# A hybrid decoder step on one core: keys of both attention maps split in one operation, and a later place for one group's weight loads

## The chip, the core and the metric

The kernel runs on one core of a Trainium2 chip. A core has five engines with instruction streams of their own: TensorE (matrix products; PE in the profile, its weight loads PEld), VectorE (DVE), ScalarE (ACT), GpSimd (POOL) and SyncE (SP), which here only issues transfers. SyncE, ScalarE and POOL can issue DMA transfers, each on a queue of its own; 16 DMA engines move the data. Each stream is worked off in order, and an instruction that waits for a semaphore holds all that stands behind it in its stream. The metric is the device time of one execution in microseconds (us), as the median of several runs. The profile is of one further execution.

## The reference

One layer of a decoder for 1024 prompt tokens and 8 sample tokens, model width 1024, all in float32: a mixer of differential attention (4 heads) and retention (4 heads) with one input and one output projection, a cross-attention to 256 memory tokens, a squared-ReLU MLP of width 4096, and a final RMSNorm. Two places matter here.

```
q1, q2 = q[..., :64], q[..., 64:]          # a head's 128 columns hold two maps
k1, k2 = k[..., :64], k[..., 64:]
attn = probs(q1, k1) - lam * probs(q2, k2) # two softmax maps, scale and bias inside
oa   = einsum('bhqk,bkhd->bqhd', attn, v)

y = square(relu(h @ w_up)) @ w_down        # hidden width 4096 = 4 groups of 1024
```

## The kernel before

**Precision.** A float32 operand is split into a high part in the format that TensorE takes at full rate (a ScalarE cast) and a low part (a VectorE subtraction, operand minus high part). A product is then high x high, high x low and low x high.

**Attention of the prompt.** TensorE's instructions are kept in the order in which they are written. A planner puts those of the other engines, transfers too, in an order by its own estimates of when each is ready; `issue_after(x)` makes an instruction stand behind x on its engine. The four heads overlap: while the scores of head h are computed, the query and key projection of head h+1 fills gaps on TensorE (`head_proj`, lines 919 to 947; it leaves keys in `kraw` and queries in `qraw`, 64 rows of map 0 above 64 rows of map 1, by 1032 columns). A loop over 44 steps (line 1369), ten to a head, says which scores, transposes and products with values come when.

`load_stacks` (949) takes the tiles of a head, one buffer each: KA[0], KA[1], KB[0], KB[1], Q[0], Q[1], each of 128 rows by 1024 columns. For map m, KA[m] is to hold the high part of the keys of that map in both of its 64-row halves, KB[m] the low part in both, and Q[m] the high part of the queries in one half and their low part in the other. So one product with KA[m] and one with KB[m] make the scores (`scores`, 999). `load_part` (961) fills columns in two calls per head: EARLY (columns 0 to 687, from step 3 of the head before) and LATE (688 to 1023, from step 7). Per map it casts 64 rows into the half of KA[m] in which they already lie, copies that half to the other by a transfer of POOL, and does the same for KB[m] with the subtraction; then both maps of Q follow. It is a generator: four pieces of it are spread over steps 3, 4, 4, 5 and 7, 7, 8, 8. Head 0 is filled ahead of the loop.

SyncE's queue in that stretch holds, in the planner's order, the bias rows of the next head (`M`), the key output, a row of norm factors of the head before and its broadcast (`norm_row`, 1098), the values of the next head, pages of the cache (`ck`), pieces of the input for the output projection (`x_half`), and more. POOL also reloads operands (`UH`, `UL`, line 1436).

**Down projection.** The hidden activations lie in DRAM as HQ and HT. For each of four groups g of 1024 hidden rows (line 2478) the product with the weights is done by seven products of half-size blocks (numbered q: 1, 2, 6, 7, 4, 5, 3), each for four column blocks p and two column chunks c, 12 matmuls of 258 columns each. `right_lower(g, q)` (2369) loads the right operand of product q in two pieces of 516 KB (`raw_h`, a ring of three buffers), casts (2381) and subtracts (2382) them into one of four slots. `load_left` (2489) loads the group's weights, two tiles of 512 KB for each p (`raw_d`, one buffer each), with the eight loads of groups 1 to 3 written ahead of that group's products; `left_lower` (2392) makes the weights of product q from them. `residual_rows` (2358) loads the rows to which results are added (`c`). In group 0 many of these stand behind named instructions; `seen["SP"]` is the last transfer that `right_lower` or `load_left` issued. The loads of group 1 have no such edge: nothing but the planner's estimate says where they go among group 0's transfers.

Of the kernel before, what the change touches and what calls it, by code (L numbers as in the profile page):

```python
# [10 lines left out]
F32 = mybir.dt.float32  # L11
# [37 lines left out]
def decoder_step(ctx: ExitStack, tc: tile.TileContext, i: dict, o: dict):  # L49
    nc = tc.nc  # L50
# [131 lines left out]
    seen = {}  # L182
# [719 lines left out]
    with pool("b") as A:  # L902
# [58 lines left out]
        def load_part(h, cs):  # L961
            KA, KB, Q, _ = stacks[h]
            qraw, kraw = raws[h]
            for m in range(2):
                own = slice(64 * m, 64 * m + 64)
                oth = slice(64 - 64 * m, 128 - 64 * m)
                nc.scalar.copy(KA[m][own, cs], kraw[own, cs])
                nc.gpsimd.dma_start(KA[m][oth, cs], KA[m][own, cs])
                nc.vector.tensor_sub(KB[m][own, cs], kraw[own, cs], KA[m][own, cs].bitcast(F32))
                nc.gpsimd.dma_start(KB[m][oth, cs], KB[m][own, cs])  # L970
                yield
            for m in range(2):
                own = slice(64 * m, 64 * m + 64)
                oth = slice(64 - 64 * m, 128 - 64 * m)
                nc.scalar.copy(Q[m][own, cs], qraw[own, cs])
                nc.vector.tensor_sub(Q[m][oth, cs], qraw[own, cs], Q[m][own, cs].bitcast(F32))
                yield

        vraws = {}
# [311 lines left out]
        for _ in load_part(0, EARLY):  # L1291
            pass
# [76 lines left out]
        for g in range(-4, 40):  # L1369
            h, x = divmod(g, 10)  # L1370
# [6 lines left out]
            if h < 3:  # L1377
                if h >= 0 and x == EARLY_AT[0]:
                    load_stacks(h + 1)
                    until(h + 1, 1, 1)  # L1380
                    early = load_part(h + 1, EARLY)
                for y in (0, 1, 2, 3):
                    if h >= 0 and x == EARLY_AT[y]:
                        if y == 2:
                            until(h + 1, 1, 0)
                        next(early)
                if x == LATE_AT[0]:
                    until(h + 1, 2, 1)
                    late = load_part(h + 1, LATE)
                for y in (0, 1, 2, 3):  # L1390
                    if x == LATE_AT[y]:
                        if y == 2:
                            until(h + 1, 2, 0)
                        next(late)
# [38 lines left out]
            while reloaded[0] < 3 and (3, reloaded[0], 0) in done:  # L1433
                cs = slice(reloaded[0] * CH, reloaded[0] * CH + CH)
# [15 lines left out]
            if g in UNITS_AT:  # L1450
                x = UNITS_OUT[len(us_out) - 1]
# [224 lines left out]
    with pool("d") as A:  # L1676
# [62 lines left out]
        for pr in range(4):  # L1739
            us = [unit(U_MQ + 2 * pr + x) for x in range(2)]  # L1740
            if pr == 0:
                seen["DVE"] = nc.cur_bb.bb.instructions[-1]
                with tc.issue_after(seen["DVE"]):
                    for c in range(2):
                        cs = slice(c * CH, c * CH + CH)
# [6 lines left out]
            for f, c in late + rest if pr else rest + late:  # L1752
                q = qm[2 * pr + f]
                cs = slice(c * CH, c * CH + CH)
# [377 lines left out]
    with pool("e") as A, pool("e_ps", space=PSUM) as PS:  # L2132
# [61 lines left out]
        for n, (ft, c) in enumerate(order):  # L2194
# [4 lines left out]
            cs = QCOLS[c]  # L2199
# [8 lines left out]
            x = xq[ft // 4, c][:, ft % 4, :]  # L2208
# [133 lines left out]
    with pool("acc", side="right") as AC, pool("rd", side="right") as RD, pool("w") as A, pool("w_ps", space=PSUM) as PS:  # L2342
# [135 lines left out]
        for g in range(4):  # L2478
# [10 lines left out]
            def load_left(pairs):  # L2489
                for p in pairs:  # L2490
                    for x in range(2):
                        nc.sync.dma_start(raws[p][x][:, :1024], i["wall"][U_DN + 8 * g + 2 * p + x])
                seen["SP"] = nc.cur_bb.bb.instructions[-1]

            load_left((0, 1) if g == 0 else range(4))
            S, W, bank, copied = {}, {}, {}, {}

            parts = [((1, 2), (1, 2), (0, 1)), ((), (1, 2), (2, 3)), ((6,), (6,), (0, 1)), ((), (6,), (2, 3))]
# [270 lines left out]
```

## Time and profile before

| | |
|---|---|
| time, median of 3 runs | 1474.56 us (1473.46 to 1474.77) |
| profiled execution | 1475.19 us, of which the span of instructions is 1473.4 |
| TensorE busy | 1455.7 us (99%), 11013 matmuls |
| VectorE, ScalarE, POOL busy | 1107.9 (75%), 679.7 (46%), 314.4 us (21%) |
| DMA | 238.98 MB, mean 162 GB/s |
| mean granted TensorE clock | 0.996 of full speed |

Times in the rows are us from the start of the span unless marked ns. A releaser behind `<-` is what ended a wait, by the semaphores. The attention of the prompt lies at about 230 to 430 us, the down projection at 1134 to 1470.

### The profile page before, as it was taken

The numbers are of one execution on the slowest core, as the hardware profiler recorded it, in microseconds if no ns is written. First come the engines' busy times: TensorE is split into PE (matmuls) and PEld (weight loads), VectorE is DVE, ScalarE is ACT, GpSimd is POOL, SyncE is SP. The second block draws the span as 40 slices with busy tenths as digits, with TensorE's granted clock in tenths as the row PEclk, the third lists the DMA queues.
The fourth block names the chain that finished last, engine by engine and source line by source line (L and its number), as shares of the span: only waits on it lengthen the run. The fifth ranks groups of instructions, "written<-read, shape, count | busy, mean of one in ns | idle before, by whom it ended". The sixth has DMA issues, their size and how long they took to land.

```text
span 1473.4 us, 28129 instructions
## 1 busy us (share of the span) xinstructions
PE 1455.7 (99%) x11013; PEld 1401.0 (95%) x11013; DVE 1107.9 (75%) x2263; ACT 679.7 (46%) x1327; POOL 314.4 (21%) x345
## 2 busy tenths in 40 slices
PE   9999999999999999999999999999999999999998
PEld 7899779999889999999999999999999999999998
DVE  7666536888867756567868988888888878787876
ACT  7434435666552441267436533343435443343454
POOL 0035433122304511224122000000002211110380
PEclk9999999999999999999999999999999999999998
DMA  8155738215957265654762444333446764536273
GB/s 295 62 188 171 205 70 192 72 34 159 283 169 269 100 209 170 177 178 122 236 234 77 151 159 158 138 136 133 149 159 216 262 213 144 173 105 200 71 130 116
DMA packets 129833, 238.98 MB, mean 162 GB/s; under 512 B 13606, under 2 KB 80987, under 8 KB 129572
## 3 DMA queue, kind: packets, MB, share of 16 engines
q1 hardware_dynamic: 91354, 170.66, 36.0%
q0 software_dynamic: 27472, 46.93, 11.8%
q10 hardware_dynamic: 10874, 19.60, 3.5%
q8 instruction: 86, 1.41, 0.4%
q14 instruction: 47, 0.39, 0.1%
HBM read 171.13 MB, written 58.92 MB: 156 GB/s over the span
## 4 chain that ended last, share of the span: by engine, by line
PE 88%; DVE 5%; DMA 2%; ACT 2%; issue 1%; POOL 0%; ACTq 0%; SPq 0%; DVEq 0%
PE dn L2412 20%; PE Z L2244 9%; PE qkp L75 6%; PE Y L2244 6%; PE X L2244 6%; PE mq L75 6%; PE pr_m L75 6%; PE pr_o L75 5%; PE grp L75 3%; PE sp L75 2%; PE mv L75 2%; PE mk L75 1%; PE av L75 1%; PE mpv L75 1%; PE vap_z L524 1%; PE vrp_z L524 1%
## 5 line engine op out<-in xcount | busy, mean ns | idle before, releaser
L2412 PE MATMUL dn<-UH,wd 128*128 128x258 f32 (+1 forms) x1800 | 326.6, 283 | 3.0 <-DVE c L2546 3.0
L2412 PEld LDWEIGHTS dn<-UH,wd 128*128 128x128 f32 x1800 | 279.6, 190 | 3.6 <-ACT wd L2388 2.6
L2412 PE MATMUL dn<-UL,wd 128*128 128x258 f32 x900 | 254.6, 283 | 0.0
L2412 PEld LDWEIGHTS dn<-UL,wd 128*128 128x128 f32 x900 | 170.5, 189 | 0.1
L2546 DVE TENSOR_TENSOR c<-c,dn 128x258 f32<-128x258 f32 (+1 forms) x217 | 89.1, 417 | 38.5 <-PE dn L2412 35.8
L2270 ACT ACTIVATE hq<-r 128x258 f32<-128x258 f32 x128 | 53.7, 421 | 117.4 <-DVE r L2269 117.3
L2244 PE MATMUL Z<-T_h,wu 128*128 128x258 f32 x512 | 98.1, 283 | 0.0
L2244 PE MATMUL X<-UH,wu 128*128 128x258 f32 x512 | 97.5, 282 | 0.0
L2388 ACT CAST wd<-raw_d 128x512 fp32r<-128x512 f32 x96 | 58.7, 619 | 82.0 <-PE dn L2412 77.3
L2052 ACT CAST wu<-raw_up 128x512 fp32r<-128x512 f32 x96 | 59.0, 616 | 61.0 <-PE Z L2244 52.6
L2381 ACT CAST UH<-raw_h 128x1032 fp32r<-128x1032 f32 x56 | 58.7, 1055 | 55.2 <-PE dn L2412 27.9
L2244 PEld LDWEIGHTS X<-UH,wu 128*128 128x128 f32 x512 | 81.3, 188 | 0.0
L2244 PEld LDWEIGHTS Z<-T_h,wu 128*128 128x128 f32 x512 | 81.3, 189 | 0.0
L2382 DVE TENSOR_TENSOR UL<-raw_h,UH 128x1032 fp32r<-128x1032 f32 x56 | 72.9, 1301 | 9.9 <-ACT UH L2381 9.9
L2389 DVE TENSOR_TENSOR wd<-raw_d,wd 128x512 fp32r<-128x512 f32 x96 | 72.3, 759 | 10.2 <-ACT wd L2388 10.2
L2281 POOL DMA_DIRECT2D HT<-ht x32 | 17.2, 536 | 292.1 <-DVE ht L2280 291.6
L2244 PE MATMUL Z<-T_l,wu 128*128 128x258 f32 x256 | 72.3, 282 | 0.0
L2244 PE MATMUL X<-UL,wu 128*128 128x258 f32 x256 | 72.3, 282 | 0.0
L129 ACT CAST wh_u<-raw_u 128x1024 fp32r<-128x1024 f32 x43 | 44.7, 1047 | 57.6 <-PE mq L75 39.9
L2053 DVE TENSOR_TENSOR wu<-raw_up,wu 128x512 fp32r<-128x512 f32 x96 | 64.8, 689 | 3.6 <-ACT wu L2052 3.6
L2402 POOL TENSOR_TENSOR raw_d<-raw_d,raw_d 128x512 f32<-128x512 f32 x16 | 22.1, 1384 | 197.0 <-DVE raw_d L2398 145.3
L130 DVE TENSOR_TENSOR wl_u<-raw_u,wh_u 128x1024 fp32r<-128x1024 f32 x39 | 48.6, 1257 | 20.2 <-ACT wh_u L129 20.0
(616 smaller groups left out, 4707.4 us busy)
## 6 DMA issues: line engine op xcount, KB each, us to landing
raw_u<-in_wall SPq DMA_DIRECT2D x49, 512.0 KB
HT<-ht POOLq DMA_DIRECT2D x32, 516.0 KB, 3.0
raw_h<-HT SPq DMA_DIRECT2D x32, 516.0 KB
raw_up<-in_wall SPq DMA_DIRECT2D x32, 512.0 KB
raw_d<-in_wall SPq DMA_DIRECT2D x32, 512.0 KB
HQ<-hq ACTq DMA_DIRECT2D x32, 387.0 KB
raw_h<-HQ SPq DMA_DIRECT2D x24, 516.0 KB
cmk<-in_cmk SPq DMA_DIRECT2D x16, 512.0 KB
```

The source lines that it names most:

```text
L75: pinned(nc.tensor.matmul(out, l, r, start=start, stop=stop))
L130: (lo_engine or nc.vector).tensor_sub(wl[:, :n], raw[:, :n], wh[:, :n].bitcast(F32))
L2052: nc.scalar.copy(w[:, :512], src)
L2053: nc.vector.tensor_sub(w[:, 512:], src, w[:, :512].bitcast(F32))
L2244: pinned(nc.tensor.matmul(ps, l, r[:, k, :], start=first and k == 0 and x == 0, stop=k == 3 and x == 2, skip_group_check=True))
L2270: nc.scalar.activation(h[:, PLACE[quad], :], r, AF.Square)
L2381: nc.scalar.copy(h, rv)
L2382: nc.vector.tensor_sub(l, rv, h.bitcast(F32))
L2388: nc.scalar.copy(w[:, :512], src)
L2389: nc.vector.tensor_sub(w[:, 512:], src, w[:, :512].bitcast(F32))
L2412: pinned(nc.tensor.matmul(ps[:, part], l, r[:, k, cq], start=first and k == 0 and x == 0, stop=k == 3 and x == 2, skip_group_check=True))
L2546: nc.vector.tensor_add(y, y, ps)
```

## The change

In `load_part`, for heads 1 to 3, one cast now fills KA[1] with all 128 rows (map 0's high part in its first half, map 1's in its second, as `kraw` has them), and one subtraction fills KB[1] in the same way. POOL copies the first half of KA[1] into both halves of KA[0], and that of KB[1] into both halves of KB[0]. Then, beside the two pieces that fill Q, SyncE copies the second half of KA[1] over its first, and that of KB[1] over its first. Head 0 is filled as before. In the down projection the eight weight loads of group 1 get an edge behind the last transfer that group 0's last `right_lower` issued.

```
         def load_part(h, cs):
             KA, KB, Q, _ = stacks[h]
             qraw, kraw = raws[h]
-            for m in range(2):
+            lo, hi = slice(0, 64), slice(64, 128)
+            if h:
+                nc.scalar.copy(KA[1][:, cs], kraw[:, cs])
+                for x in (lo, hi):
+                    nc.gpsimd.dma_start(KA[0][x, cs], KA[1][lo, cs])
+                nc.vector.tensor_sub(KB[1][:, cs], kraw[:, cs], KA[1][:, cs].bitcast(F32))
+                yield
+                for x in (lo, hi):
+                    nc.gpsimd.dma_start(KB[0][x, cs], KB[1][lo, cs])
+                yield
+            for m in range(0 if h else 2):
                 own = slice(64 * m, 64 * m + 64)
                 oth = slice(64 - 64 * m, 128 - 64 * m)
                 nc.scalar.copy(KA[m][own, cs], kraw[own, cs])
...
                 nc.scalar.copy(Q[m][own, cs], qraw[own, cs])
                 nc.vector.tensor_sub(Q[m][oth, cs], qraw[own, cs], Q[m][own, cs].bitcast(F32))
+                if h:
+                    K1 = (KA, KB)[m][1]
+                    nc.sync.dma_start(K1[lo, cs].bitcast(F32), K1[hi, cs].bitcast(F32))
                 yield
...
                         nc.sync.dma_start(raws[p][x][:, :1024], i["wall"][U_DN + 8 * g + 2 * p + x])
                 seen["SP"] = nc.cur_bb.bb.instructions[-1]
 
-            load_left((0, 1) if g == 0 else range(4))
+            with tc.issue_after(seen["SP"]) if g == 1 else nullcontext():
+                load_left((0, 1) if g == 0 else range(4))
             S, W, bank, copied = {}, {}, {}, {}
```

## Rows read from the trace of the kernel before

**Rows 1.** Table of stretches: us, busy time (count) of five engines, clock, DMA share, GB/s.
```profile
308.00:353.00 45.00, 44.01 (x304) 42.62 (x303) 37.66 (x104) 26.88 (x60) 11.05 (x20) 1.00 0.44 118
353.00:398.00 45.00, 42.57 (x311) 39.78 (x310) 39.03 (x106) 28.12 (x62) 14.85 (x25) 1.00 0.84 233
1190.00:1195.00 5.00, 5.00 (x35) 5.00 (x34) 2.59 (x5) 2.42 (x3) 0.00 (x0) 0.74 1.01 341
1200.00:1300.00 100.00, 100.00 (x837) 100.00 (x836) 83.48 (x137) 38.16 (x53) 16.66 (x13) 1.00 0.47 144
```

**Rows 2.** Timeline, TensorE, group 0: start, us, instruction, count, idle before and its releaser.
```profile
1188.26 0.36 PE L2412 MATMUL dn<-UH,wd 128*128 128x258 f32 x1 [2.38 <-DVE c L2546]
...
1189.17 0.41 PE L2412 MATMUL dn<-UL,wd 128*128 128x258 f32 x1
...
1192.39 0.37 PE L2412 MATMUL dn<-UL,wd 128*128 128x258 f32 x1
```

**Rows 3.** Chain of waits, end of group 0: start, us, what.
```profile
1163.76 3.88 DMA raw_h<-HT
...
1177.60 7.84 DMA raw_h<-HQ
...
1185.46 1.06 ACT UH L2381
...
1186.55 1.23 DVE UL L2382
```

**Rows 4.** Timeline, SyncE's transfers at the end of group 0.
```profile
1170.42 0.97 SPq L2492 DMA_DIRECT2D raw_d<-in_wall  x2
1174.51 0.38 SPq L2375 DMA_DIRECT2D raw_h<-HQ  x1
1174.93 0.51 SPq L2492 DMA_DIRECT2D raw_d<-in_wall  x1
...
1178.02 3.34 SPq L2361 DMA_DIRECT2D c<-X  x4
...
1186.93 8.36 SPq L2375 DMA_DIRECT2D raw_h<-HQ  x4
1195.87 0.34 SPq L2492 DMA_DIRECT2D raw_d<-in_wall  x1
```

**Rows 5.** Timeline, ScalarE, a cast for group 1's first right operand.
```profile
1194.09 1.06 ACT L2381 CAST UH<-raw_h 128x1032 fp32r<-128x1032 f32 x1
```

**Rows 6.** Views by line, key split: ns min/median/max, first and last start, forms; landing.
```profile
L967 ACT CAST KA<-kraw x16: 467/614/768, 240.9 to 378.9; 64x688 fp32r<-64x688 f32 x8, 64x336 fp32r<-64x336 f32 x8
...
L969 DVE TENSOR_TENSOR KB<-kraw,KA x16: 500/682/879, 241.7 to 379.7; 64x688 fp32r<-64x688 f32 x8, 64x336 fp32r<-64x336 f32 x8
...
DMA to landing us min/median/max: 2.2/4.9/7.8
```

**Rows 7.** Chain of waits, attention, head 3.
```profile
379.96 5.82 DMA rbh<-hrow
```

**Rows 8.** Timeline, ScalarE, second key cast of head 3's first part.
```profile
367.62 0.76 ACT L967 CAST KA<-kraw 64x688 fp32r<-64x688 f32 x1
```

**Rows 9.** Timeline, POOL, last key transfer of head 3's first part.
```profile
372.77 0.54 POOL L970 DMA_DIRECT2D KB<-KB  x1
```

**Rows 10.** Timeline, TensorE, first products of head 3 with low keys, map 0 and 1.
```profile
378.37 0.28 PE L75 MATMUL sp<-KB,Q 128*128 128x256 f32 x1
...
381.88 0.28 PE L75 MATMUL sp<-KB,Q 128*128 128x256 f32 x1
```

**Rows 11.** Timeline, SyncE, attention, head 3.
```profile
377.03 0.33 SPq L1105 DMA_DIRECT2D hrow<-hr  x1
...
385.12 1.71 SPq L1342 DMA_DIRECT2D x_half<-in_xT  x3
```

**Rows 12.** Timeline, VectorE, first use of x_half.
```profile
393.68 0.51 DVE L1356 TENSOR_TENSOR x_half<-pr_half,x_half 128x344 f32<-128x344 f32 x1
```

**Rows 13.** SyncE's waits, 360 to 400 us: total, times, longest, in us.
```profile
SPq L1105 <- ACT hr L1104: 10.7, 1, 10.7
```

## The prediction

> **What bounds the kernel now.** I read the table of stretches first, because the share of busy time over the whole span hides where TensorE stands still. In [rows 1] TensorE is busy for all of 1200 to 1300 us at a granted clock of 1.00 and starts 837 matmuls, 119.5 ns each; nothing but a stop of TensorE can be won or lost there. The two attention stretches of the table, 308 to 353 and 353 to 398 us (keys of heads 2 and 3), hold 0.99 and 2.43 us of idle TensorE, 3.42 us together. Next I read TensorE's timeline of the first group of the down projection: one stop of 2.38 us ends at 1188.26 [rows 2], the largest of the whole span. After it the granted clock falls, 0.74 on the mean of 1190 to 1195 [rows 1]: the 15 matmuls that start from 1189.17 up to 1192.39 take 3.22 us [rows 2], where 15 at 119.5 ns take 1.79. So the stop costs 2.38 + 1.43 = 3.81 us. From 1188.26 to the end TensorE hardly stops again, so an earlier start there is an earlier end.
>
> The chain of waits says what the stop waited for. It runs from a raw_h transfer issued at 1177.60, which took 7.84 us, through the ScalarE cast (1.06) and the VectorE subtraction (1.23), to TensorE [rows 3]. That is the second piece of the right operand of product 3, the last operand of group 0. The same kind of transfer took 3.88 us when it was issued at 1163.76 [rows 3]. SyncE's timeline shows the difference: ahead of the two pieces of product 3 (issued at 1174.51 and 1177.60) stand two raw_d loads from 1170.42 on, and a third at 1174.93 [rows 4]. They are left weights of group 1, 512 KB each, which nobody needs before group 1.
>
> **Part 1: the left weights of group 1 go behind the last operand of group 0.** Removed from in front of the two pieces: three loads, 1.5 MB. Price of the wait as it is: 7.84 us for the second piece. Price without them: at best the 3.88 us of the transfer at 1163.76, which also had a load issued right behind it; at worst no change, if the four residual loads at 1178.02 (1 MB, still directly behind the second piece) [rows 4] are what slows it. I take 3.88, the row of the same transfer, since the loads that move are issued before the pieces and the residual loads after. Then the second piece lands at 1177.60 + 3.88 = 1181.48, is cast and subtracted by 1183.8, and with the 0.5 us of VectorE addition and issue that the chain shows between subtraction and matmul TensorE could go on at 1184.3. Its previous matmul ends at 1188.26 - 2.38 = 1185.88. The stop is gone with 1.6 us to spare, and with no stop I expect no fall of the clock: -3.81 us.
>
> What is late next? The moved loads. The four of the first two pairs can go out at about 1181.4, behind the residual loads, and then hold the DMA engines: 2 MB at the 341 GB/s of [rows 1] is about 6 us. The first right operand of group 1, issued from 1186.93 on [rows 4], is pushed by some 1.5 us; its second piece is cast at 1194.09 [rows 5], so at about 1195.6, subtracted by 1198. Group 1 starts 144 matmuls after 1188.26: at 1185.88 + 144 x 0.1195 = 1203.1 when the stop is gone. About 5 us are spare, and the first weights land before that operand. If that cover were gone, each us late would stop TensorE for one us.
>
> **Part 2: one split for both maps, heads 1 to 3.** Each head is loaded in two parts (688 and 336 columns). Per part one ScalarE copy and one VectorE subtraction go: 3 x (0.77 + 0.47) = 3.7 us of ScalarE and 3 x (0.87 + 0.50) = 4.1 us of VectorE [rows 6]. The pair that stays covers 128 partitions and the same columns; I cost it as before. Bounds of this relief: at most the 3.42 us of idle TensorE in [rows 1], at least nothing. I take nothing: VectorE has gaps between the removed subtractions and these stops, and the chain into the largest of them starts at a broadcast load [rows 7], not at a key.
>
> Added per part: POOL still issues four transfers, SyncE two more, twelve in all. Each head's path gets longer. The one copy writes the second map's tile, so it can't start before the last product of the head before has read it; I put it where the second copy stood, for head 3 at 367.62 [rows 8]. From there: copy 0.76, subtraction 0.87, two issues of 0.54 on POOL [rows 9], landing 4.9 (2.2 to 7.8) [rows 6]. The low halves of map 0 are there at 367.62 + 0.76 + 0.87 + 1.08 + 4.9 = 375.2; the first product with them is at 378.37 [rows 10]. SyncE then copies inside the second map's tile, issue and landing about 5 us more: 380.4, against 381.88 [rows 10]. Both are in time, by 3.2 and 1.5 us. With every landing at 7.8 they would be 378.1 and 386.3, 4.4 us too late; with every landing at 2.2 nothing is gained. The value is 0, by the median row. Heads 1 and 2 have the same distances within a us.
>
> The twelve waits on SyncE hold what is queued behind them: for head 3's first part the row of norm factors at 377.03, for its last part the cache loads and the three x_half loads at 385.12 [rows 11]. The former is not due until 1.8 us after the copy goes out. The latter could go out 3 us late if POOL's last transfer of that part, issued about 380.5, takes the longest landing (388.3); VectorE first reads them at 393.68 [rows 12], 8.6 us after their issue. I cost it 0, and 2 us at worst.
>
> The Trainium skill, page "DMA: Bandwidth & Descriptors", section "Issuing engines are not separate DMA queues", says that transfers begun by different engines run on the same 16 DMA engines, and a second issuer saves only its issue time. By it the SyncE copies would not run beside POOL's for nothing: head 3's 512 KB would take 2.2 us at the 233 GB/s of its stretch. The DMA share of 0.84 there [rows 1] agrees that little is free; the sum by it would be -1.6 us if all of that reached TensorE.
>
> **Sum.** -3.81 (stop and clock) + 0 (keys) = -3.8. The profiled execution took 1475.19 us (span 1473.4 and 1.8 around it), 0.63 above the median of 1474.56; it would become 1471.4, and the median 1470.8.
>
> **Rivals.**
> B, the stop shrinks only. The residual loads behind the second piece share the DMA engines with it. For: its transfer took twice the time of the one at 1163.76. Against: that one had a load behind it too. If it takes 5.9 us, halfway, TensorE goes on at 1186.3: idle 0.4 us, with part of the clock loss: about -2.4, 1472.2.
> C, the wait moves to group 1. SyncE takes its instructions in order; the right operands of group 1 may be planned behind all eight weight loads, of which one before the last went out only at 1195.87, when its buffer came free [rows 4]. With operand pieces from 1196.5 on, 5 us to land beside the other loads and 2.8 for cast, subtraction and issue, TensorE starts group 1 at 1204.3, 1.2 us late: -2.6, 1472.0. Against: before, the planner put four operand pieces ahead of that load [rows 4].
> D, the other side: SyncE is held by the second map's copy of head 3 past 377.03. If POOL's low halves go out only where the last of them went before, at 372.77 behind a reload of another operand [rows 9], and take the longest landing of 7.8 [rows 6], they are there at 380.6; SyncE then sends the norm row there instead of 377.03, its broadcast, now issued at 379.96 and 5.82 us long [rows 7], comes 3.6 us later, and VectorE waits for it ahead of the scores. TensorE stops for 3.6 us and loses the clock for 1.4 more: +5.0 - 3.8 = +1.2, 1475.8. It decides once the hold is over 2.4 us. SyncE's waits bear out the mechanism: it stood 10.7 us for the source of that norm row [rows 13], and issued nothing meanwhile.
> The Trainium skill, page "DMA: Bandwidth & Descriptors", section "Anatomy of one DMA — SWDGE (gpsimd) path", says that a semaphore is waited for on the issuing sequencer, before dispatch; by that rule D's hold is real, and the trace agrees, by the 10.7 us just named.
> E, the relief counts: fewer VectorE instructions let the stops of heads 2 and 3 shrink by some 1.5 us: 1469.3.
> F, the change doesn't do what it says: with the edge the planner sets other transfers of group 1 in front of the two pieces, and the second still takes some 7.8 us: 1474.6.
>
> **Chances.** Forecast 0.55 (its own range 1469.5 to 1472.1: half of the 2.43 us of [rows 1] to either side), B 0.13, C 0.06, D 0.11, E 0.10, F 0.05. The range for 8 in 10 reaches from 1469.0, just under E, over B, C and F to 1474.8; D and what lies beyond either end are left out. About 0.2%, 2.9 us, is what a measurement of this kernel can tell from no change, so the border of faster is 1471.6: most of the forecast (0.46), E (0.10) and a little of B give 0.57 faster; the rest of the forecast, B, C, F and half of D give 0.36 the same; D with a larger hold, or with F, gives 0.07 slower.
>
> **What would show it.** Right: after the change SyncE issues both pieces of product 3 before any raw_d of group 1; the second piece takes about 4 us; no stop near 1185 and a clock of 1.00 there; ScalarE with 6 casts fewer and VectorE with 6 subtractions fewer; the two attention stretches with about the same 3.4 us of idle TensorE. Wrong: a stop at the first product of group 1 (C), or stops above 5 us in the attention stretches that end on a broadcast, an x_half load or a key tile (D).

## The result: slower by 0.27%, and where the profile after puts it

| | before | changed |
|---|---|---|
| median of 10 runs each | 1473.3 us (1472.09 to 1475.1) | 1477.65 us (1476.26 to 1478.93) |
| ratio, 95% interval | | 1.0027 (1.0019 to 1.0035) |
| profiled execution, span | 1475.19, 1473.4 | 1478.3, 1476.6 |

The forecast was 1470.8 us and its range ended at 1474.8. It started from the 1474.56 us of three runs; ten runs of the same kernel have a median of 1473.3. A second set of 11 runs of the changed kernel gave 1.0022 (1.0013 to 1.0031). The change costs some 3 to 4 us. Of the runs named below, one of 2845.15 us (copies on POOL) and one of 6725.12 us (x_half on ScalarE) are slow ones and count neither in the ratios nor in the medians.

The table of stretches of the changed kernel (columns as in [rows 1]) shows both parts of the change at work:

```profile
308.00:353.00 45.00, 43.93 (x302) 42.51 (x301) 36.24 (x102) 25.86 (x58) 11.30 (x19) 1.00 0.48 125
353.00:398.00 45.00, 41.66 (x305) 38.89 (x303) 35.51 (x100) 25.65 (x58) 14.89 (x25) 0.99 0.88 237
398.00:430.00 32.00, 31.39 (x273) 27.62 (x272) 26.61 (x63) 18.38 (x32) 0.93 (x5) 0.96 0.72 241
1190.00:1195.00 5.00, 4.82 (x40) 4.65 (x39) 4.01 (x10) 1.24 (x2) 0.00 (x0) 1.00 0.97 347
1200.00:1300.00 100.00, 98.33 (x815) 97.65 (x814) 84.09 (x134) 40.34 (x55) 15.88 (x12) 1.00 0.50 153
```

Three rows differ from before. From 1190 to 1195 us the clock is 1.00 (the upper of its two levels, 2.4 GHz, throughout) instead of 0.74: the stop of 2.38 us and the low clock behind it are gone. From 1200 to 1300 us TensorE, which had stood nowhere, stands for 1.67 us. From 353 to 398 us it stands for 3.34 us instead of 2.43, and a clock of 0.96 follows, where this profile of the kernel before had 1.00:

```profile
398.00:430.00 32.00, 31.39 (x283) 27.78 (x283) 25.92 (x61) 17.94 (x32) 2.42 (x6) 1.00 0.70 229
```

By these shares the lower clock takes some 1.7 us of full clock away (an estimate: 0.01 of 45 us and 0.04 of 32 us).

TensorE executes the same 11013 matmuls in the same order in both kernels (and in all that follow), so the start of the n-th one can be set against the start of the n-th before. (The times that follow are those of the matmuls in the kernel before.) Up to the one at 300 us the changed kernel is 0.1 us late; over the next 140 us it loses 2.1 us more, around 630 to 655 us another 1.8, and 0.4 where the down projection begins; late in group 0, from 1188.26 to 1192.6, it wins 3.7, as forecast (3.81); then it gives back 2.7 up to 1226. It ends 3.4 us late.

**Head 3.** SyncE's timeline, changed kernel:

```profile
380.64 0.32 SPq L1123 DMA_DIRECT2D rbh<-hrow  x1
381.05 0.39 SPq L996 DMA_DIRECT2D vraw<-out_v_p  x1
382.53 0.91 SPq L989 DMA_DIRECT2D KA<-KA  x1
386.25 0.47 SPq L989 DMA_DIRECT2D KB<-KB  x1
387.73 2.91 SPq L874 DMA_DIRECT2D ck<-in_cache_kT  x4
390.74 1.37 SPq L1355 DMA_DIRECT2D x_half<-in_xT  x3
```

The second copy of the last part (386.25) stood until POOL's transfer of the low half had landed; behind it stood the cache loads and the x_half loads, which went out at 390.74 instead of 385.12 [rows 11]. The chain of waits goes on from there:

```profile
390.74 5.29 DMA x_half<-in_xT
...
396.12 0.22 DVE x_half L1369
...
396.55 0.76 DVE e L1047
```

```profile
396.12 0.52 DVE L1369 TENSOR_TENSOR x_half<-pr_half,x_half 128x344 f32<-128x344 f32 x1 [2.15 <-DMA x_half<-in_xT]
```

VectorE stood 2.15 us at the x_half addition, which in the kernel before it ran at 393.68 [rows 12], and the attention weights queued behind it came late. TensorE's timeline has the stop there: 2.58 us, where the kernel before had one of 1.40 at the same matmul. First the line of before, then those of the changed kernel:

```profile
395.97 0.55 PE L78 MATMUL trA<-ident,e 128*128 128x128 f32 x3 [1.40 <-DVE e L1034]
```

```profile
397.35 0.89 PE L78 MATMUL trA<-ident,e 128*128 128x128 f32 x3 [2.58 <-DVE e L1047]
...
1190.50 0.36 PE L2425 MATMUL dn<-UH,wd 128*128 128x258 f32 x1 [0.18 <-DVE c L2560]
...
1207.41 0.39 PE L2425 MATMUL dn<-UH,wd 128*128 128x258 f32 x1 [0.76 <-DVE c L2560]
...
1215.45 0.36 PE L2425 MATMUL dn<-UH,wd 128*128 128x258 f32 x1 [0.59 <-DVE c L2560]
```

From 300 to 440 us the stops of TensorE above 0.12 us add up to 4.98 us, against 4.27 before. The longer standing is thus 0.7 of the 2.1 us lost there; the rest came with the lower clock behind the stop.

**Groups 0 and 1.** The stop of 2.38 us [rows 2] is down to 0.18. SyncE's timeline shows both operand pieces of product 3 ahead of every raw_d, as forecast, and then the price: six loads ahead of group 1's first operand piece, and one more, waiting for its buffer, ahead of the second and of the third piece.

```profile
1179.21 2.87 SPq L2388 DMA_DIRECT2D raw_h<-HQ  x2
1182.13 2.86 SPq L2374 DMA_DIRECT2D c<-X  x4
1185.04 4.91 SPq L2505 DMA_DIRECT2D raw_d<-in_wall  x6
1190.00 1.24 SPq L2388 DMA_DIRECT2D raw_h<-HQ  x1
1195.02 0.33 SPq L2505 DMA_DIRECT2D raw_d<-in_wall  x1
1195.40 0.43 SPq L2388 DMA_DIRECT2D raw_h<-HQ  x1
1197.92 0.33 SPq L2505 DMA_DIRECT2D raw_d<-in_wall  x1
1198.30 4.94 SPq L2388 DMA_DIRECT2D raw_h<-HQ  x2
```

The first piece took from 1190.00 to 1200.52 to its cast on ScalarE. VectorE's timeline shows who stood for it:

```profile
1201.61 1.23 DVE L2395 TENSOR_TENSOR UL<-raw_h,UH 128x1032 fp32r<-128x1032 f32 x1 [3.23 <-ACT UH L2394]
1202.76 0.42 DVE L2560 TENSOR_TENSOR c<-c,dn 128x258 f32<-128x258 f32 x1
...
1204.75 2.27 DVE L2395 TENSOR_TENSOR UL<-raw_h,UH 128x1032 fp32r<-128x1032 f32 x1
1206.95 0.41 DVE L2560 TENSOR_TENSOR c<-c,dn 128x258 f32<-128x258 f32 x1
```

VectorE stood 3.23 us for the operand of group 1, and the subtraction of its second piece took 2.27 us instead of 1.23. The additions that evict group 0's finished sums (c<-c,dn) were queued behind these subtractions; one of them ended at 1207.36, and TensorE, which writes its next sums into the bank that this addition empties, went on at 1207.41. A group is 672 matmuls, and group 1 begins at 1221.28 here. So the stops of 0.76 and 0.59 us lie in the last product of group 0 (product 3, 108 and 48 matmuls ahead of group 1); only a third, of 0.32 us at 1229.07, lies in group 1. It is an eviction that is late, not an operand.

The stop of 2.38 us before was of the same kind. It stands at the 433rd matmul of group 0, where product 4 adds to banks that product 7 has filled 48 matmuls earlier; product 3, whose operand the chain of [rows 3] loads, begins 96 matmuls later. VectorE's timeline before:

```profile
1183.87 1.23 DVE L2382 TENSOR_TENSOR UL<-raw_h,UH 128x1032 fp32r<-128x1032 f32 x1 [4.69 <-ACT UH L2381]
...
1187.70 0.42 DVE L2546 TENSOR_TENSOR c<-c,dn 128x258 f32<-128x258 f32 x1
```

VectorE stood 4.69 us for the first piece of that operand, then subtracted the second [rows 3], and the eviction that TensorE waited for came last, ending at 1188.12.

### The profile page after: what moved, and what is told of

Read it like the earlier page. It is cut to its first block, busy times and chain, and to the rows that moved or that the text cites. A ratio compares the mean times of both kernels' runs of the same rounds, so it can differ in the third digit from the quotient of the medians.

```text
span 1476.6 us, 28140 instructions
## 1 busy us (share of the span) xinstructions
PE 1457.1 (99%) x11013; PEld 1401.5 (95%) x11013; DVE 1103.9 (75%) x2257; ACT 675.9 (46%) x1321; POOL 311.6 (21%) x345
## 4 chain that ended last, share of the span: by engine, by line
PE 83%; DVE 8%; DMA 5%; ACT 2%; issue 2%; ACTq 0%; SPq 0%; POOL 0%; DVEq 0%
PE dn L2425 17%; PE Z L2257 9%; PE qkp L75 7%; PE pr_m L75 6%; PE X L2257 6%; PE Y L2257 6%; PE mq L75 5%; PE pr_o L75 5%; PE grp L75 3%; PE sp L75 2%; PE av L75 2%; DMA raw_u<-in_wall 1%; PE mpv L75 1%; DMA raw_h<-HQ 1%; PE vap_z L524 1%
## 5 line engine op out<-in xcount | busy, mean ns | idle before, releaser
L75 PE MATMUL qkp<-UH,wh_u 128*128 128x344 f32 x192 | 62.9, 327 | 0.1
```

The source lines that it names most:

```text
L75: pinned(nc.tensor.matmul(out, l, r, start=start, stop=stop))
```

## Experiments

The theory at this point: the keys cost by SyncE's hold in head 3, the edge wins 3.7 us and gives 2.7 back ("the stops in group 1" of the texts below are those from 1200 us on, most of which lie in the last product of group 0). The rivals: the losses are the execution's chance, or they belong to the other part.

Each kernel's profile is one more execution of the stretches that its edit does not touch. So all are read in one table: how long TensorE took from its matmul no. 1940 to no. 2948 (300.21 to 440.08 us before: keys of heads 2 and 3), and from no. 8317 to no. 9124 (1139.04 to 1240.03: groups 0 and 1). Both columns are differences of two starts on TensorE's timeline. The last column is the ratio of times to the kernel before, run on the same chip.

```
kernel                           300-440  1139-1240  ratio (95%)
before, first profile             139.88    100.99
before, second profile            140.47     98.25
edge alone                        139.68     97.17   1.0006 (0.9996 to 1.0017)
edge, operands behind all loads   140.93     98.88   1.0000 (0.9991 to 1.0009)
edge, pairs 2, 3 behind operands  140.87     98.22   1.0002 (0.9991 to 1.0012)
edge on pairs 2, 3 only           139.24     97.50   0.9994 (0.9985 to 1.0003)
  the same again                  140.97     97.77   0.9999 (0.9991 to 1.0008)
changed                           142.02    100.30   1.0027 (1.0019 to 1.0035)
changed, again                    142.25     99.45   1.0022 (1.0013 to 1.0031)
changed, head 3 as before         139.67    101.25   1.0016 (1.0006 to 1.0027)
keys alone                        141.67     97.56   1.0014 (1.0005 to 1.0024)
keys alone, copies on POOL        142.39     98.03   1.0023 (1.0013 to 1.0033)
SyncE's hold alone                142.02     97.77   1.0023 (1.0014 to 1.0032)
keys alone, x_half on ScalarE     145.43     98.52   1.0040 (1.0026 to 1.0054)
```

### The edge alone

The kernel before with the change's last hunk only:

```diff
-            load_left((0, 1) if g == 0 else range(4))
+            with tc.issue_after(seen["SP"]) if g == 1 else nullcontext():
+                load_left((0, 1) if g == 0 else range(4))
```

> The kernel before with the edge on the left loads alone; the keys are split as before. Theory A (the profile's account): the edge takes 3.7 us off at the end of group 0 and 2.7 us come back in group 1, because four loads of pairs 2 and 3 go out ahead of the second operand of group 1; net -1.0, 1472.3 us beside 1473.3. Rival A1 (the give-back belongs to the shift that the keys bring along, not to the order of the loads): -3.7, 1469.6, with no stop in group 1. Both expect no loss in the stretch of head 3 (380 to 400 us) and none at 630 to 660 us.

Measured: 1474.73 us, ratio 1.0006. Its profiled execution (1472.11 us) is one of the shortest of its 12. In it no stop in groups 0 and 1 is above 0.15 us; the stretch is the shortest of all, 97.17. VectorE stood only 0.86 and 0.61 us for group 1's first operand, whose first piece came in 9.3 us instead of 10.5. Yet the median of its 12 runs gains nothing: a gain of 3.7 us (0.9975) lies outside the interval. The time fits neither theory, and the next kernel shows why.

### The keys alone

The changed kernel without that hunk.

> The split of the keys alone; the left loads of group 1 are issued as before. Theory A: +2.4 us in the stretch of head 3 up to 435 us (SyncE held by the copies of the last part, the x_half loads late) and +0.5 ahead of it; the 1.7 us lost at 630 to 655 us follow from the shift and come again: 1477.6 to 1478 us, the stop of 2.4 us near 1188 unchanged. Rival A2 (the 1.7 us at 630 to 655 us are chance of one execution): 1476.2 with that stretch as in the kernel before.

Measured: 1475.94 us, 1.0014, near rival A2's 1476.2. The stretch of head 3 lost 1.8 us again; the loss at 630 to 655 us came half (0.9). But the stop near 1188, which this kernel should have kept whole, was 0.46 us with the clock at 1.00: in the same order of transfers, the stretch took 97.56 us instead of 100.99.

### The kernel before, a second profile

> The kernel before, unchanged, for a second profile of it. Theory A (the stop of 2.38 us at 1188 is one draw of a transfer that shares the DMA engines; the kernel with only the keys changed, same order there, showed 0.46): the second piece of product 3 takes 6 to 8 us and the stop lies between 0 and 2.4 us, with other stops of 0.3 to 1.5 us elsewhere that the first profile lacks. Rival A7 (the stop belongs to the kernel): 2.2 to 2.5 us again.

Measured: TensorE's timeline, and the chain that ends in the stop:

```profile
1189.38 0.36 PE L2412 MATMUL dn<-UH,wd 128*128 128x258 f32 x1 [0.58 <-DVE c L2546]
```

```profile
1180.94 5.62 DMA raw_h<-HQ
...
1186.58 1.07 ACT UH L2381
...
1187.67 1.23 DVE UL L2382
```

The same piece took 5.62 us, not the 7.84 of [rows 3], the stop 0.58 instead of 2.38, and the table of stretches gives the clock there as 1.00 instead of 0.74:

```profile
1190.00:1195.00 5.00, 5.00 (x44) 5.00 (x44) 2.37 (x6) 0.94 (x1) 0.00 (x0) 1.00 1.04 373
```

In four executions with this order of transfers (this one, keys alone, POOL's copies, the hold) the stop is 0.58, 0.46, 0.42 and 0.60 us, and a fifth (x_half on ScalarE) has none. The 2.38 of the first profile, and with it the 1.43 us of low clock, was one draw of six. Rival A7 falls.

### Head 3 as before

```diff
-            if h:
+            if h in (1, 2):
                 nc.scalar.copy(KA[1][:, cs], kraw[:, cs])
...
-            for m in range(0 if h else 2):
+            for m in range(0 if h in (1, 2) else 2):
...
-                if h:
+                if h in (1, 2):
                     K1 = (KA, KB)[m][1]
```

> Both parts of the change, but head 3 splits its keys as before: SyncE's copies are gone from 373 to 387 us. Theory A (the loss is the hold of SyncE in head 3): the 2.4 us of that stretch go, about 0.5 for heads 1 and 2 and -1.0 for the edge stay: 1472.8 us, or 1474.5 if the loss at 630 to 655 us comes again. Rival A3 (the longer path of the keys costs in every head, VectorE's and POOL's order in heads 1 and 2 shift the rest): at least 2 us of the loss stay by 435 us: 1475 to 1476.5.

Measured: 1475.33 us, 1.0016. The loss of 300 to 440 us is gone (139.67), and the stop is that of the kernel before:

```profile
395.52 0.55 PE L78 MATMUL trA<-ident,e 128*128 128x128 f32 x3 [1.41 <-DVE e L1047]
```

So heads 1 and 2 cost nothing in that stretch, and A3 falls by its condition, though the time lies in A3's range and above the 1472.8 to 1474.5 of theory A; this profile lost 3.0 us against the second one of before in groups 0 and 1 (stops of 0.37 us at 1188.22, of 0.44, 0.59 and 0.31 us after VectorE had stood 2.80 for group 1's first operand, and one of 1.52 at 1141.62, where the down projection begins).

### The hold alone

The kernel before, with two transfers that nothing reads:

```diff
+    held = dram.tile([2, 64, 344], F32, tag="held", name="held")
...
                 nc.vector.tensor_sub(Q[m][oth, cs], qraw[own, cs], Q[m][own, cs].bitcast(F32))
+                if h == 3 and cs == LATE:
+                    nc.sync.dma_start(held[m, :, : cs.stop - cs.start], (KA, KB)[m][1][0:64, cs].bitcast(F32))
```

> The kernel before, keys split as before; added are only two transfers on SyncE that read the second map's key halves of head 3's last part (into a scratch in DRAM that nothing reads), where the change has its copies: the wait for POOL's landings without the new split. Theory A: SyncE is held to about 387.5 us, x_half goes out near 391 instead of 385, VectorE stands at the x_half addition, and TensorE loses 1.7 to 2.4 us by 440 us: 1475.0 to 1475.7. Rival A5: the hold is harmless, below 0.5 us: 1473.3 to 1473.8.

Measured: 1476.8 us, 1.0023 (2.1 to 4.7 us). All other engines have the instructions of the kernel before, in their order; SyncE's order differs, besides the two transfers, only behind the x_half loads. SyncE's timeline, VectorE's and TensorE's:

```profile
384.82 0.50 SPq L979 DMA_DIRECT2D held<-KA  x1
386.42 0.46 SPq L979 DMA_DIRECT2D held<-KB  x1
387.93 3.66 SPq L875 DMA_DIRECT2D ck<-in_cache_kT  x4
391.69 1.33 SPq L1345 DMA_DIRECT2D x_half<-in_xT  x3
```

```profile
395.42 0.52 DVE L1359 TENSOR_TENSOR x_half<-pr_half,x_half 128x344 f32<-128x344 f32 x1 [1.53 <-DMA x_half<-in_xT]
```

```profile
396.65 0.79 PE L78 MATMUL trA<-ident,e 128*128 128x128 f32 x3 [1.96 <-DVE e L1037]
```

The x_half load itself took 3.7 us here (391.69 to 395.42), less than the 5.29 in the changed kernel, so its late issue and not the added bytes made it late. The wait on SyncE is enough by itself for the loss in this stretch, at the same matmul and of the same size (142.02). The time is above what theory A gave: three of the 12 runs, the profiled one among them, took 1473.3 to 1474.1 us and the other nine 1476.3 to 1478.6, and no profile shows where the nine lose the rest.

### The copies on POOL

```diff
-                    nc.sync.dma_start(K1[lo, cs].bitcast(F32), K1[hi, cs].bitcast(F32))
+                    nc.gpsimd.dma_start(K1[lo, cs], K1[hi, cs])
```

Keys alone, without the edge.

> The split of the keys alone, with the copies inside the second map's tile issued by POOL instead of SyncE; the left loads of group 1 as before. Theory A (the loss of the keys is SyncE's hold ahead of the x_half loads): x_half is issued near 385.5 us again, the 1.8 to 2.1 us between 370 and 440 us of the trace are gone, at most 0.5 remain: 1473.5 to 1474 us beside 1473.3 of the kernel before. Rival A5 (the longer path of the low halves itself, or POOL's six issues, are late): the stretch still loses 1.5 us or more, on a key tile or on an operand reload of POOL: 1475 to 1476.

Measured: 1476.49 us, 1.0023: theory A's 1473.5 to 1474 was wrong. x_half went out at 386.75, and the loss came all the same (142.39), on another chain:

```profile
376.81 4.55 DMA hrow<-hr
...
381.38 6.05 DMA rbh<-hrow
...
387.45 0.69 DVE oraw L1150
```

The row of norm factors took 4.55 us to land, where the kernel before took some 3 (377.03 to the broadcast at 379.96, [rows 7, 11]); TensorE stopped 1.57 us at 389.38 for the weights behind it. All stops of the stretch together are 4.41 us, hardly more than before; most of the loss is the clock, 0.93 from 353 to 398 us. SyncE has no hold here. What made the row's landing long is not shown: POOL has six transfers where there were four, and its reloads of operands went out 1.2 us later than in the changed kernel (from 373.69 instead of 372.48), nearer to the row. Two chains end nearly together at this point, the x_half loads and the broadcast, and in the profiles taken the split delays one or the other.

### x_half issued by ScalarE

```diff
-                    nc.sync.dma_start(xc, i["xT"][:, ft, cs])
+                    (nc.scalar if n < 3 else nc.sync).dma_start(xc, i["xT"][:, ft, cs])
```

Keys alone, SyncE's copies as in the change.

> The split of the keys alone, SyncE's copies as in the change, but the first three x_half loads are issued by ScalarE, so that SyncE's hold can't delay them; the left loads as before. It adds about 1.2 us of issue to ScalarE. Theory A (the hold of the x_half loads is the loss): they go out near 386 us, and the stretch from 370 to 440 us loses at most 0.7 us (1.8 to 2.1 with SyncE): 1474 to 1474.7. Rival A12 (the added transfers themselves, by the broadcast of the norm factors, as the kernel with POOL's copies showed with 4.55 us for the row's landing instead of 3.1): 1.3 us or more stay, on the chain of that broadcast: 1475.3 to 1476.5.

Measured: 1478.28 us (median of five runs), 1.0040, worse than either said. The chain of waits and TensorE's timeline:

```profile
382.49 6.34 DMA KA<-KA
...
388.85 5.97 DMA x_half<-in_xT
...
394.84 0.06 ACT ah L1065
```

```profile
395.86 1.06 PE L1224 MATMUL dsc<-ck,qblkd 128*16 128x128 f32 x16 [6.41 <-ACT qblkd L1201]
```

The second x_half load waited on ScalarE until 388.83 for the landing of SyncE's key copy, ScalarE's next cast until 394.82 for the landing of that load: it stood 7.5 us, six of them for the load. It does not tell A from A12; it shows a hold on a queue where more waits behind it.

### Operands ahead of the loads of pairs 2 and 3

```diff
+            with tc.issue_after(seen["SP"]) if g == 1 else nullcontext():
+                load_left((0, 1) if g < 2 else range(4))
...
                     S.update({q: right_lower(g, q) for q in new})
+                    if g == 1 and 1 in new:
+                        with tc.issue_after(seen["SP"]):
+                            load_left((2, 3))
```

> The keys as before; the edge holds only the loads of pairs 0 and 1, and those of pairs 2 and 3 go out behind both operands of group 1 that its first products need. Theory A (the four loads ahead of the second operand make the stops in group 1): no stop at the products with that operand, the whole gain stays: -3.7, 1469.6 us. Rival A4 (the bytes are the limit: eight loads that start late push the operands in whatever order): stops in group 1 of 1 to 2 us stay, at an operand or at a left weight of pair 2: 1471 to 1472.3.

Measured: 1473.74 us, 1.0002, one stop of 0.23 us at 1202.92, though VectorE stood 3.21 us for the first operand here too. The stops shrink as A said; the gain of 3.7 isn't there, since the stop of 2.38 us that it was to come from was a draw.

### Operands behind all eight loads

The edge alone, and group 1's first operands behind the last of the loads:

```diff
+                elif g == 1 and 1 in new:
+                    with tc.issue_after(seen["SP"]):
+                        S.update({q: right_lower(g, q) for q in new})
```

> The keys as before, the edge on all eight left loads as in the change, and the operands of group 1's first products behind all eight (the change has the second operand behind six to eight of them, the first behind six). Theory A (the give-back in group 1 is the loads ahead of the operands): the last piece of the second operand is cast at least 1 us later than in the kernel with the edge alone (1201.7), and TensorE stops 1.5 to 4 us in group 1: 1475.5 to 1478 us. Rival A11 (the stops of group 1 are draws that have nothing to do with that order): stops of 0 to 1 us, 1474 to 1474.7 as the edge alone.

Measured: 1473.63 us, 1.0000. The last piece was cast at 1209.71, 8.0 us later than with the edge alone (5.0 against TensorE's own progress), and TensorE's stops were 0.62 and 0.32 us. A was right on the delay and wrong on its price; the stops are those of A11. VectorE stood only 0.59 us here: with the operand planned that late, its subtraction was planned behind the evictions. So how late the operand comes does not decide by itself. Nor does how long VectorE stands for it: in the six executions with the order of before it stood 2.4 to 3.4 us for that operand, up to 1193.7 to 1198.7 (1201.6 in the changed kernel), with no stop behind it, and with operands ahead of the loads of pairs 2 and 3 it stood 3.21 us for a stop of 0.23. Every stop from 1200 us on ends on an eviction; which of the waits and subtractions ahead of it make it late is not shown.

### Only pairs 2 and 3 wait, twice

The same as the one with the operands first, but pairs 0 and 1 without the edge.

> The keys as before; the left loads of pairs 0 and 1 of group 1 go out where the planner likes, as before, and only those of pairs 2 and 3 wait, behind both operands of group 1. Of the three loads around the pieces of product 3 one leaves (that between the two pieces). Theory A: the second piece lands in 5 to 6 us (6.3 and 7.9 with three loads, 4.1 to 4.3 with none), the stop near 1188 shrinks to 0 to 0.5 us, and group 1 has no stop, since its operands go out earlier than before: 1470.5 to 1472. Rival A6 (the two loads ahead of the first piece are what slows both): the second piece still takes 6 to 8 us, stop 0.5 to 2.4: 1473 to 1473.5.

> The edge on the loads of pairs 2 and 3 alone, behind both operands of group 1, a second time, for a narrower interval (0.9994 of the kernel before, 0.9985 to 1.0003). Theory A (it takes away the stop of 0.4 to 0.6 us that four of five executions show near 1188, and the larger one that some show, and stops nothing in group 1): 0.5 to 1.5 us below the kernel before: 1472 to 1473. Rival A10 (a draw): within 0.3 us of the kernel before: 1473.2 to 1473.7.

Measured: 1472.51 us, 0.9994, and 1473.0 us, 0.9999. The second piece took 4.4 and 5.2 us to its cast; the stop near 1188 was nil and 0.26; no stop in group 1. This is the best of all, and no measurable gain.

### The change, a second profile

> The changed kernel, unchanged, for a second profile and beside the others of this group. Theory A: x_half goes out near 391 us again and the stretch from 370 to 440 us loses 1.7 to 2.4 us again, since SyncE's hold is in the program; the second piece of product 3 takes 4.1 to 4.3 us again; the stops of group 1 (0.76, 0.59 and 0.32 us in the first profile) are draws and lie between 0 and 2 us together. Time 1476 to 1478 us. Rival A9 (the first profile's losses are all draws): the stretch from 370 to 440 us loses less than 0.7 us: 1474 to 1475.

Measured: 1478.03 us, 1.0022. x_half went out at 391.24; VectorE stood 2.48 us for group 1's first operand; two of TensorE's stops:

```profile
397.62 0.55 PE L78 MATMUL trA<-ident,e 128*128 128x128 f32 x3 [2.50 <-DVE e L1047]
...
1216.01 0.36 PE L2425 MATMUL dn<-UH,wd 128*128 128x258 f32 x1 [0.58 <-DVE c L2560]
```

The stretch lost 2.4 us again: the loss of head 3 belongs to the program, and A9 falls.

## Why the prediction was wrong

Two steps failed: the price of the stop in part 1, and the hold costed at nothing in part 2.

**Part 1, the term of -3.81.** This step failed by its size: with no load of group 1 around them, the second piece reached its cast in 3.9 to 4.3 us in six executions, against 3.88 forecast; with three loads it took 5.6 to 7.9 in six. So the loads do slow the pieces, as forecast. But "The stop is gone with 1.6 us to spare, and with no stop I expect no fall of the clock: -3.81 us" takes the price from one execution. In five others with the same order the stop is 0 to 0.60 us and the clock stays at 1.00: what there was to win is some 0.5 us. Over 1139 to 1240 the five took 98.0 us on the mean, the profile on which the forecast stood 101.0. Nothing in that profile says that its stop is rare; the medians, close to its own time, hid it, because its other stretches were lucky (the second profile of the same kernel has the same span and lost 2.7 us more in them). The prediction also took the stop for one at product 3. TensorE waited for an eviction that stood behind the operand's subtraction on VectorE, 96 matmuls before product 3; the 0.5 us that it counted as the way from subtraction to matmul is that eviction.

**"About 5 us are spare" in group 1.** Wrong three times. The pieces were forecast 1.5 us later; with the edge alone the second piece of the first operand was cast at 1197.46, 3.4 later than in [rows 5], in the changed kernel at 1203.26. SyncE stood for two buffers (1195.02 and 1197.92) with operand pieces behind: that is the mechanism of rival C, which had 0.06, though TensorE never stopped at the first product of group 1. Group 1 begins 240 matmuls behind the stop, not 144 (at 1218.57 in the profile before), so TensorE's own cover was 11.5 us longer than stated, here and in rival C's price. And it did not help, since I asked when TensorE needs the operand; VectorE meets it first, with evictions behind. In the four executions with the change's order of these transfers VectorE stood there 1.5, 2.5, 2.8 and 3.2 us, and TensorE's stops from 1200 us on were 0, 1.0, 1.3 and 1.7. They took 97.2, 99.5, 101.3 and 100.3 us, 99.5 on the mean, 1.5 above the 98.0. So the edge gains nothing (1.0006, 0.9996 to 1.0017); that it costs is likely by the profiles and not shown by the times.

**Part 2, the hold costed at 0.** This is the other step that failed: "I cost it 0, and 2 us at worst." The mechanism, its queue and its victim stood in the prediction; the judgment was made with the longest landing as the exception. No long landing was needed: SyncE was held to 386.25 by a landing of 5.5 us after POOL's issue, four cache loads followed, and x_half came 5.6 us late against a cover put at 8.6. The "3 us late" let x_half go out the moment the hold ends (388.3 against 385.12) and left out the copy and the four cache loads between, 4.5 us of SyncE's time (386.25 to 390.74). The cover was counted from issue to first reading, as if the load took no time: the loads took 5.29 us, so 3.3 were spare. From 300 to 440 us the first seven executions of the table took 140.3 us on the mean (139.24 to 140.97), the changed kernel 142.02 and 142.25, keys alone 141.67: 1.7 us. With head 3 as before it was 139.67, with the hold alone 142.02. The 1.7 us have two parts. The stops of the stretch add up to 4.9 us on the mean of four profiles with SyncE's hold (changed twice, keys alone, hold alone: 4.55 to 5.32) and to 4.0 in the eight without hold or split in head 3 (3.51 to 4.79). And the clock falls to its lower level (1.2 GHz) for a time between 353 and 430 us in all six profiles with the split in head 3 or the hold, against three of these eight. Without the hold, on POOL, the split lost as much, by the broadcast and the clock; no version of it that was run was free. The Trainium skill, page "DMA: Bandwidth & Descriptors", section "Issuing engines are not separate DMA queues", says that transfers begun by another engine still run on the same DMA engines; by that rule POOL's copies share these engines with the norm row, and the trace agrees with that as far as one landing can, by the 4.55 us of that row.

**What held.** ScalarE's key casts went from 16 to 10 and VectorE's subtractions likewise, at unchanged durations (median 0.61 and 0.69 us with 128 partitions); in no run did the relief shorten the stretch of heads 2 and 3 (E falls). Rival D had the right kind of mechanism and sign (SyncE in order, 1475.8), at the wrong victim: the norm row left at 377.52, 0.5 us later. The key tiles themselves were in time.

**The sum.** Head 3 +1.7 and the edge 0 to +1.5 make +1.7 to +3.2 against 4.0 (2.8 to 5.2) and 3.2 (1.9 to 4.6) measured. The 1.8 us at 630 to 655 us came wholly, half or hardly in other kernels. Against the first profile of before, from 620 to 660 us, the six profiles with the new split lose 0.7 to 1.8 us (1.0 on the mean), the seven others without it 0.0 to 0.8 (0.4 on the mean). So some 0.6 us may belong to the split; no run was made for it alone, and it stays open. The hold alone measured 2.1 to 4.7 us where its stretch shows 1.7; that remainder is not explained.

## What to carry to other kernels

A stop that ends on a DMA in one profiled execution may be a draw: before a change is priced by it, look for the same order of transfers in another execution, or take the price from the shortest and the longest landing of that kind in the trace. A wait put on a queue is paid by whatever stands behind it, and the cover to subtract from is first use minus issue minus the transfer's own time. Loads moved out of one operand's way go in front of the next one. And when a wait for an operand is priced, ask which engine meets it first: here VectorE did, with evictions behind, long before TensorE needed the operand.

## What was not expected of the hardware

The same transfer, in the same place of the same program, took 5.62 us in one execution and 7.84 in another, and a stop of 2.38 us was followed by a granted clock of 0.74 where stops of 0.4 to 0.6 us were followed by 1.00. A stop of 0.26 us at 765 to 771 us, near none of the edits, was followed by a fall of the clock in five of the 14 profiles and by none in the others; the five lost 1.5 to 2.5 us from 700 to 900 us, the others at most 1.0. Medians over 10 to 12 runs told kernels apart to some 1.3 us; single profiles of this kernel differed by 3 us in one stretch of 100.
